# Value products of grouped query attention: one product for the two heads of a pair

## The chip, the cores and the metric

The program runs on one core of a Trainium2 chip. The metric is device time in microseconds, the median of the runs; lower is better. Engines go by the profile's names: PE is the matrix engine (PEld its weight loads), DVE the vector engine, ACT the scalar engine, POOL GpSimd, SP the engine whose queue issues the DMAs here.

## What is computed

Two layers over 512 latent tokens with 256 context tokens in front of them, model width 1024, all in fp32. Each layer projects its input with one large matrix, runs four mixers (a state-space scan S5, a short convolution, neighbourhood attention NA, grouped query attention GQA), gates each branch, projects it to the model width ("merge"), sums the branches, and projects the sum once more. In GQA there are 8 query heads of 64 and 2 key/value heads, so four query heads share the values of one key/value head:

```python
def block(i):                       # 128 queries, a window of 384 keys, and 256 context keys
    s_lat = jnp.where(ok, jnp.einsum("bqkgd,bskd->bkgqs", q_i, k_i) * scale, NEG_INF)
    s_ctx = jnp.einsum("bqkgd,bckd->bkgqc", q_i, k_ctx) * scale
    pr = jax.nn.softmax(jnp.concatenate([s_lat, s_ctx, sink_l], axis=-1), axis=-1)
    o = (jnp.einsum("bkgqs,bskd->bqkgd", pr[..., :span], v_i)
         + jnp.einsum("bkgqc,bckd->bqkgd", pr[..., span:span + n_ctx], v_ctx))
```

The last two lines are the value products that the change touches. Context queries see context keys only. Layer 0 computes latent and context outputs (768 tokens), layer 1 latent ones alone (512).

## The kernel before

**Arithmetic.** An fp32 product is made of three reduced-precision ones: each operand is split into a high part (an ACT cast, L229) and a low part (a DVE subtraction, L230), and hi x hi, hi x lo and lo x hi are summed in PSUM. The large projections ("dense" work) do this at L209: a unit is a weight tile of 128x1024 (`wraw`, two buffers, loaded by SP at L170), cast by ACT (`whi`, L177) and subtracted by DVE or POOL (`wlo`, L178); then come 24 matmuls of 512 columns into `pl` for the latent tokens, and in layer 0 another 24 of 256 columns into `pc` for the context.

**Attention.** `attend_` handles 128 queries of one head: logits into PSUM tile `S` (one buffer, shared with the merges), a bias and row maximum on DVE, the exponential on ACT (L579), normalisation on DVE, then PE transposes of the probabilities into `T` (two buffers, L590), split into `ph` and `pl_` (two buffers each). The value product follows at once: for each block of 128 keys three matmuls of 64 weight columns and 128 moving columns into `M` (L599), after which ACT copies `M` into `y` (L617). `gqa_tiles` goes head by head: for each of the two heads of a pair four latent blocks, in layer 0 two context blocks. There are 48 such head-blocks of GQA in layer 0 and 32 in layer 1; NA has as many.

**Order.** A layer's `front` weaves the attention tiles of eight pairs (m = 0 to 3 NA, 4 to 7 GQA) with dense units; a scheduler then sets each engine's order by priorities, with `attend` raised by `tile_prio` = 1500. In layer 0, `s5_prep` (DVE work for the S5 branch) is woven into pairs 6 and 7. After the last pair, `gate(7)` closes the front: POOL multiplies the gate with `y` (L414), ACT and DVE split it (`ghi`, `glo`), SP stores both to DRAM (L422, L423). The `back` begins with `merge`: SP loads the gated branches again as `gh` and `gl` (L1315, eight loads), PE multiplies them into `S` (L209, named `S<-gh`, `S<-gl`), DVE adds the result to `acc` (L1335), and since `S` has one buffer the second merge waits for that. In layer 0 the first steps of the S5 back (`sX`, `swin`, `sWO` on DVE, L1025 to L1043; their PE transposes L1060 and L1069) stand between the first and the second merge. SP runs its queue in order: the stores of `gate(7)`, weight loads, the S5 loads (`skl`, `smt`, `su`) and the `gh`/`gl` loads stand behind each other.

Of the kernel before, what the change touches and what calls it, by code (L numbers as in the profile page):

```python
# [12 lines left out]
F32R = mybir.dt.float32r  # L13
AF = mybir.ActivationFunctionType
OP = mybir.AluOpType
# [5 lines left out]
CTX = 256  # L21
# [9 lines left out]
C_BADA, C_G, C_CONVB, C_CONVW, C_NAQ, C_NAK, C_GQQ, C_GQK, C_SINK, N_COLS = 0, 24, 32, 36, 48, 49, 50, 51, 52, 60  # L31
B_S5, B_CONV, B_NA, B_GQA = 0, 1, 2, 3

NA_KEYS = [(0, (2, 3)), (1, (6, 7)), (3, (7, 8)), (4, (4, 5))]
# [88 lines left out]
class Net:  # L123
# [424 lines left out]
    def attend(self, *args):  # L548


        with self.tc.high_priority(offset=self.tile_prio):
            self.attend_(*args)

    tile_prio = 1500

    def attend_(self, pool, qs, kh, kl, v, qtok, k0, vbs, bias, sink, dst):
        nc = self.nc
        n = len(vbs) * 128
        S = self.ps.tile([128, 1024], F32, name="S")
# [19 lines left out]
        nc.scalar.activation(s[:, a:e], s[:, a:e], AF.Exp, bias=tn[:, 1:2], accum_out=tn[:, 2:3])  # L579
        nc.vector.reciprocal(tn[:, 3:4], tn[:, 2:3])  # L580
        nc.vector.tensor_scalar(s[:, a:640], s[:, a:640], tn[:, 3:4], None, op0=OP.mult)
        ph = pool.tile([128, 640], F32R, name="ph", bufs=2)
        pl = pool.tile([128, 640], F32R, name="pl_", bufs=2)
        vbs = (*vbs, 0, 1)
        nb = len(vbs)
        for b0 in range(0, nb, 4):
            b1 = min(nb, b0 + 4)
            T = self.ps.tile([128, 512], F32, name="T", bufs=2)
            for b in range(b0, b1):
                nc.tensor.transpose(T[:, (b - b0) * 128:(b - b0 + 1) * 128], s[:, a + b * 128:a + (b + 1) * 128], self.ident)  # L590
            c = slice(b0 * 128, b1 * 128)
            self.split(ph[:, c], pl[:, c], T[:, :(b1 - b0) * 128])
        o = self.ps.tile([128, 512], F32, name="M")
        i = 0
        for b in range(nb):
            vb = vbs[b]
            c = slice(b * 128, (b + 1) * 128)
            for w, p in ((slice(0, 64), ph), (slice(0, 64), pl), (slice(64, 128), ph)):
                last = nc.tensor.matmul(o[:64, :128], v[:, vb, w], p[:, c], start=i == 0, stop=i == 3 * nb - 1)  # L599
                i += 1  # L600
        self.last_pv = last.ins
        dst(o[:64, :128])

    def store_y(self, y, h, j, na):
        nc = self.nc
        part = y[h * 64:(h + 1) * 64]

        def f(o):
            a = CTX - self.base
            if j < 0:  # L610
                d = part[:, (j + 2) * 128:(j + 3) * 128]
            elif na:
                d = part[:, a:].rearrange("p (r b c) -> p b r c", r=8, b=8)[:, 2 * j:2 * j + 2]
                o = o.rearrange("p (b r c) -> p b r c", r=8, c=8)
            else:
                d = part[:, a + j * 128:a + (j + 1) * 128]
            nc.scalar.copy(d, o)  # L617
        return f

    def na_setup(self, pool):  # L620
        self.biases, self.nbias = [], 0
        for i in range(2):
            b = pool.tile([128, 640], F32, name=f"bias{i}")
            self.nc.gpsimd.memset(b[:, 384:], 0.0)
            self.biases.append(b)
# [9 lines left out]
    def na_tiles(self, l, pool, m, parts, A):  # L635
        nc = self.nc
        A["y"] = y = self.tp(pool, "y", bufs=2)
        for h in range(2):
            args = (pool, A["qs"][h], A["kh"][h], A["kl"][h], A["v"][:, :, h])
            for j in range(4):  # L640
                b = self.biases[self.nbias % 2]
                self.nbias += 1
                k0, vbs = NA_KEYS[j]
                nc.sync.dma_start(b[:, 128:384], self.ap["bias"][l, 2 * m + h, j])
                self.attend(*args, CTX + j * 128, k0, vbs, b[:, 128:], None, self.store_y(y, h, j, True))
                yield
            if "c" in parts:
                for j in (-2, -1):
                    self.attend(*args, (j + 2) * 128, 0, (), self.zeros, None, self.store_y(y, h, j, True))
                    yield  # L650
        self.dump(f"yna{l}{m}", y)

    def gqa_k(self, l, pool, A):
# [7 lines left out]
    def gqa_tiles(self, l, pool, m, parts, A):  # L661
        A["y"] = y = self.tp(pool, "y", bufs=2)
        kv = m // 2
        for h in range(2):
            sink = self.cols[:, l, C_SINK + 2 * m + h:C_SINK + 2 * m + h + 1]
            args = (pool, A["qs"][h], A["kh"][kv], A["kl"][kv], A["v"][:, :, kv])
            for j in range(4):
                k0, k1 = max(0, j - 1), min(4, j + 2)
                mask = self.gmask3 if j == 3 else self.gmask[:, 128 if j == 0 else 0:]
                self.attend(*args, CTX + j * 128, 2 * k0, range(2 + k0, 2 + k1), mask, sink, self.store_y(y, h, j, False))  # L670
                yield
            if "c" in parts:
                for j in (-2, -1):
                    self.attend(*args, (j + 2) * 128, 0, (), self.zeros, sink, self.store_y(y, h, j, False))
                    yield
        self.dump(f"ygq{l}{m}", y)

    def front(self, l, pool, parts):
# [784 lines left out]
```

## Time and profile before

| | |
|---|---|
| median of 3 runs | 2170.95 us (2165.61 to 2174.13) |
| the profiled execution: its own time, its span | 2171.66 us, 2169.9 us |
| PE busy, of the span | 2097.1 us, 97% |
| DVE, ACT, POOL busy | 62%, 41%, 15% |
| chain that ended last, share of PE | 65% |
| clock of PE granted, mean | 0.976 of full |

The page gives busy times, the span in slices, the chain of waits followed back from the last instruction, and groups of instructions by line. A matmul's duration in a timeline is longer than its distance to the next one, since matmuls overlap in the pipeline; what one costs the engine is that distance, called its slot below.

### The profile page before, as it was taken

How to read it: one execution, taken by the hardware profiler on the slowest of the kernel's cores; microseconds unless marked ns; L12 is line 12 of the kernel's file. 1: busy time of each engine (PE TensorE's matmuls, PEld its weight loads, DVE VectorE, ACT ScalarE, POOL GpSimd, SP SyncE). 2: the span in 40 equal slices, each digit the busy share in tenths (PEclk: the TensorE clock that was granted, in tenths of full speed). 3: DMA queues.
4: the chain of work that ended last, by engine and by line, in shares of the span. 5: the costliest groups of instructions: out<-in, count | busy, mean ns of one | idle time of the engine just before them, and what ended most of it. 6: DMA issues, size and time to landing. Idle time of an engine off the chain costs nothing.

```text
span 2169.9 us, 34654 instructions
## 1 busy us (share of the span) xinstructions
PE 2097.1 (97%) x12868; PEld 1792.5 (83%) x12868; DVE 1351.5 (62%) x2770; ACT 898.5 (41%) x1936; POOL 322.3 (15%) x326
## 2 busy tenths in 40 slices
PE   8899999899999999999799998999999999999999
PEld 3788888798898888888688887888888887778877
DVE  6476767579665777777457764555556655556543
ACT  3454444354643333333233345555545443223332
POOL 1722122232310000000000003222223300000000
PEclk9999999999999999999899998999999999999999
DMA  6453553532324565554164765444333328764452
GB/s 254 129 151 103 154 151 112 156 120 64 135 81 156 149 179 161 135 178 126 54 205 142 219 208 183 136 118 131 98 112 96 110 95 259 232 199 135 144 167 97
DMA packets 165773, 316.45 MB, mean 146 GB/s; under 512 B 59362, under 2 KB 83170, under 8 KB 164836
## 3 DMA queue, kind: packets, MB, share of 16 engines
q1 hardware_dynamic: 165604, 314.24, 47.1%
q8 instruction: 101, 1.65, 0.3%
q14 instruction: 68, 0.56, 0.1%
HBM read 214.09 MB, written 51.31 MB: 122 GB/s over the span
## 4 chain that ended last, share of the span: by engine, by line
PE 65%; DMA 6%; DVE 5%; ACT 2%; SPq 1%; issue 1%; POOL 0%; DVEq 0%; ACTq 0%; POOLq 0%
PE pl L209 34%; PE pc L209 10%; PE S L209 8%; PE M L599 3%; DMA s<-s 2%; PE T L590 2%; PE T L1069 1%; PE S L563 1%; PE S L565 1%; PE T L1143 1%; DMA gl<-gd 1%; DMA gd<-s 1%; PE M L478 1%; PE T L1060 1%; DMA s<-yd 1%
## 5 line engine op out<-in xcount | busy, mean ns | idle before, releaser
L209 PE MATMUL pl<-hh,whi 128*128 128x512 f32 x1312 | 526.5, 403 | 5.4 <-ACT hh L229 2.5
L209 PE MATMUL pl<-hh,wlo 128*128 128x512 f32 x1312 | 525.3, 400 | 6.1 <-DVE wlo L178 6.1
L209 PE MATMUL pl<-hl,whi 128*128 128x512 f32 x1312 | 525.0, 400 | 0.4 <-DVE hl L230 0.4
L177 ACT CAST whi<-wraw 128x512 fp32r<-128x512 f32 x440 | 272.4, 622 | 534.7 <-PE pl L209 190.5
L178 DVE TENSOR_TENSOR wlo<-wraw,whi 128x512 fp32r<-128x512 f32 x348 | 241.4, 696 | 185.0 <-ACT whi L177 178.1
L209 PEld LDWEIGHTS pl<-hh,wlo 128*128 128x128 f32 x1312 | 249.4, 190 | 60.9 <-DVE wlo L178 8.2
L209 PEld LDWEIGHTS pl<-hh,whi 128*128 128x128 f32 x1312 | 249.8, 191 | 56.2 <-ACT hh L229 3.7
L209 PEld LDWEIGHTS pl<-hl,whi 128*128 128x128 f32 x1312 | 249.6, 190 | 51.0 <-DVE hl L230 1.5
L209 PE MATMUL pc<-hh,whi 128*128 128x256 f32 x768 | 225.4, 294 | 10.4 <-ACT hh L229 5.0
L209 PE MATMUL pc<-hl,whi 128*128 128x256 f32 x768 | 223.0, 290 | 0.7 <-DVE hl L230 0.5
L209 PE MATMUL pc<-hh,wlo 128*128 128x256 f32 x768 | 222.2, 289 | 0.0
L178 POOL TENSOR_TENSOR wlo<-wraw,whi 128x512 fp32r<-128x512 f32 x92 | 128.0, 1394 | 314.0 <-ACT whi L177 273.5
L209 PEld LDWEIGHTS pc<-hh,whi 128*128 128x128 f32 x768 | 149.1, 194 | 19.4 <-ACT hh L229 6.0
L579 ACT ACTIVATE s<-s,stiny 128x512 f32<-128x512 f32 (+2 forms) x160 | 112.8, 705 | 112.3 <-DVE stiny L578 56.0
L209 PEld LDWEIGHTS pc<-hl,whi 128*128 128x128 f32 x768 | 149.2, 194 | 6.8 <-DVE hl L230 1.6
L599 PE MATMUL M<-ph,v 128*64 128x128 f32 x1216 | 147.2, 228 | 4.1 <-ACT y L617 1.8
L209 PEld LDWEIGHTS pc<-hh,wlo 128*128 128x128 f32 x768 | 149.3, 194 | 0.8 <-issue 0.4
L209 PE MATMUL S<-gh,whi 128*128 128x512 f32 (+1 forms) x384 | 139.0, 362 | 3.0 <-DVE mt L1335 1.6
L209 PE MATMUL S<-gl,whi 128*128 128x512 f32 (+1 forms) x384 | 137.5, 358 | 1.6 <-DMA gl<-gd 1.6
L209 PE MATMUL S<-gh,wlo 128*128 128x512 f32 (+1 forms) x384 | 137.2, 357 | 0.0
L599 PEld LDWEIGHTS M<-ph,v 128*64 128x64 f32 x1216 | 127.0, 138 | 11.7 <-ACT y L617 3.1
L229 ACT CAST ph<-T 128x512 fp32r<-128x512 f32 (+2 forms) x192 | 92.8, 497 | 56.5 <-PE T L590 49.7
(778 smaller groups left out, 3738.4 us busy)
## 6 DMA issues: line engine op xcount, KB each, us to landing
wraw<-wu SPq DMA_DIRECT2D x220, 512.0 KB
wada<-wada SPq DMA_DIRECT2D x40, 512.0 KB
s<-s SPq DMA_DIRECT2D x80, 192.0 KB
bias<-bias SPq DMA_DIRECT2D x64, 128.0 KB
kh<-qhi SPq DMA_DIRECT2D x40, 192.0 KB
kl<-qlo SPq DMA_DIRECT2D x40, 192.0 KB
gh<-gd SPq DMA_DIRECT2D x16, 384.0 KB
gl<-gd SPq DMA_DIRECT2D x16, 384.0 KB
```

The lines of the kernel that those rows point to most:

```text
L177: nc.scalar.copy(hi, raw[:, c])
L178: e.tensor_tensor(lo, raw[:, c], hi.bitcast(F32), op=OP.subtract)
L209: mm = nc.tensor.matmul(out[q], a[:, c], b[k][:, s], start=k + n == 0, stop=k == nk - 1 and n == 2)
L229: self.nc.scalar.copy(hi, src)
L478: nc.tensor.matmul(sums[:, 2 * b:2 * b + 2], sq[:, c:c + 128], self.blk1, start=True, stop=True)
L563: nc.tensor.matmul(S[:, 512 - n:512], qa, k[:, CTX + k0 * 64:CTX + k0 * 64 + n], start=i == 0, stop=i == 1)
L565: nc.tensor.matmul(S[:, 512:768], qa, k[:, :CTX], start=i == 0, stop=i == 1)
L579: nc.scalar.activation(s[:, a:e], s[:, a:e], AF.Exp, bias=tn[:, 1:2], accum_out=tn[:, 2:3])
L590: nc.tensor.transpose(T[:, (b - b0) * 128:(b - b0 + 1) * 128], s[:, a + b * 128:a + (b + 1) * 128], self.ident)
L599: last = nc.tensor.matmul(o[:64, :128], v[:, vb, w], p[:, c], start=i == 0, stop=i == 3 * nb - 1)
L1060: nc.tensor.transpose(o[:, g * 128:(g + 1) * 128], win[d][:, g].rearrange("p s i -> p (s i)"), self.ident)
L1069: nc.tensor.matmul(o[:16, g * 128:(g + 1) * 128], X[:, 0, d, g], WO[:, d, g, d:d + 8].rearrange("p k i -> p (k i)"), start=True, stop=True)
```

## The change

In GQA the two heads of a pair are done side by side, block by block: `gqa_tiles` now loops over the query block outside and the head inside, and after the second head one call (`values_`) does the value products of both. The weights are the high and low halves of the values together (128 columns), the moving operand is the probabilities of both heads together (256 columns), first their high part and then their low part: two matmuls for each block of keys instead of three for each head. Rows 0 to 63 of the result hold what came from the high values, rows 64 to 127 what came from the low ones (the product lo x lo is thereby added). ACT copies the first half of a head into `y` as before, and DVE then adds the second half (new, L631). `ph` and `pl_` become one tile each for the whole front, with two halves: a GQA pair uses both halves at once, NA alternates between them. The products of NA keep their form.

```diff
--- before.py
+++ after.py
@@ -551,9 +551,13 @@
         with self.tc.high_priority(offset=self.tile_prio):
             self.attend_(*args)
 
+    def values(self, *args):
+        with self.tc.high_priority(offset=self.tile_prio):
+            self.values_(*args)
+
     tile_prio = 1500
 
-    def attend_(self, pool, qs, kh, kl, v, qtok, k0, vbs, bias, sink, dst):
+    def attend_(self, pool, qs, kh, kl, half, qtok, k0, vbs, bias, sink):
         nc = self.nc
         n = len(vbs) * 128
         S = self.ps.tile([128, 1024], F32, name="S")
@@ -579,10 +583,8 @@
         nc.scalar.activation(s[:, a:e], s[:, a:e], AF.Exp, bias=tn[:, 1:2], accum_out=tn[:, 2:3])
         nc.vector.reciprocal(tn[:, 3:4], tn[:, 2:3])
         nc.vector.tensor_scalar(s[:, a:640], s[:, a:640], tn[:, 3:4], None, op0=OP.mult)
-        ph = pool.tile([128, 640], F32R, name="ph", bufs=2)
-        pl = pool.tile([128, 640], F32R, name="pl_", bufs=2)
-        vbs = (*vbs, 0, 1)
-        nb = len(vbs)
+        ph, pl = (t[:, half] for t in self.pt)
+        nb = len(vbs) + 2
         for b0 in range(0, nb, 4):
             b1 = min(nb, b0 + 4)
             T = self.ps.tile([128, 512], F32, name="T", bufs=2)
@@ -590,23 +592,33 @@
                 nc.tensor.transpose(T[:, (b - b0) * 128:(b - b0 + 1) * 128], s[:, a + b * 128:a + (b + 1) * 128], self.ident)
             c = slice(b0 * 128, b1 * 128)
             self.split(ph[:, c], pl[:, c], T[:, :(b1 - b0) * 128])
+
+    def values_(self, v, vbs, half, dsts):
+
+
+        nc = self.nc
+        ph, pl = self.pt
+        vbs = (*vbs, 0, 1)
         o = self.ps.tile([128, 512], F32, name="M")
-        i = 0
-        for b in range(nb):
-            vb = vbs[b]
+        for b, vb in enumerate(vbs):
             c = slice(b * 128, (b + 1) * 128)
-            for w, p in ((slice(0, 64), ph), (slice(0, 64), pl), (slice(64, 128), ph)):
-                last = nc.tensor.matmul(o[:64, :128], v[:, vb, w], p[:, c], start=i == 0, stop=i == 3 * nb - 1)
-                i += 1
+            if half is None:
+                for i, p in enumerate((ph, pl)):
+                    last = nc.tensor.matmul(o[:, :256], v[:, vb], p[:, :, c], start=b + i == 0, stop=b == len(vbs) - 1 and i == 1)
+                continue
+            for i, (w, p) in enumerate(((slice(0, 64), ph), (slice(0, 64), pl), (slice(64, 128), ph))):
+                last = nc.tensor.matmul(o[:64, :128], v[:, vb, w], p[:, half, c], start=b + i == 0, stop=b == len(vbs) - 1 and i == 2)
         self.last_pv = last.ins
-        dst(o[:64, :128])
+        for h, dst in enumerate(dsts):
+            dst(o[:, h * 128:(h + 1) * 128], half is None)
 
     def store_y(self, y, h, j, na):
         nc = self.nc
         part = y[h * 64:(h + 1) * 64]
 
-        def f(o):
+        def f(o, two):
             a = CTX - self.base
+            o, o2 = o[:64], o[64:]
             if j < 0:
                 d = part[:, (j + 2) * 128:(j + 3) * 128]
             elif na:
@@ -615,10 +627,13 @@
             else:
                 d = part[:, a + j * 128:a + (j + 1) * 128]
             nc.scalar.copy(d, o)
+            if two:
+                nc.vector.tensor_tensor(d, d, o2, op=OP.add)
         return f
 
     def na_setup(self, pool):
         self.biases, self.nbias = [], 0
+        self.pt = [pool.tile([128, 2, 640], F32R, name=n) for n in ("ph", "pl_")]
         for i in range(2):
             b = pool.tile([128, 640], F32, name=f"bias{i}")
             self.nc.gpsimd.memset(b[:, 384:], 0.0)
@@ -635,19 +650,23 @@
     def na_tiles(self, l, pool, m, parts, A):
         nc = self.nc
         A["y"] = y = self.tp(pool, "y", bufs=2)
+        half = 0
         for h in range(2):
-            args = (pool, A["qs"][h], A["kh"][h], A["kl"][h], A["v"][:, :, h])
-            for j in range(4):
-                b = self.biases[self.nbias % 2]
-                self.nbias += 1
-                k0, vbs = NA_KEYS[j]
-                nc.sync.dma_start(b[:, 128:384], self.ap["bias"][l, 2 * m + h, j])
-                self.attend(*args, CTX + j * 128, k0, vbs, b[:, 128:], None, self.store_y(y, h, j, True))
+            v = A["v"][:, :, h]
+            for j in (0, 1, 2, 3) + ((-2, -1) if "c" in parts else ()):
+                args = (pool, A["qs"][h], A["kh"][h], A["kl"][h], half)
+                if j >= 0:
+                    b = self.biases[self.nbias % 2]
+                    self.nbias += 1
+                    k0, vbs = NA_KEYS[j]
+                    nc.sync.dma_start(b[:, 128:384], self.ap["bias"][l, 2 * m + h, j])
+                    self.attend(*args, CTX + j * 128, k0, vbs, b[:, 128:], None)
+                else:
+                    vbs = ()
+                    self.attend(*args, (j + 2) * 128, 0, vbs, self.zeros, None)
+                self.values(v, vbs, half, (self.store_y(y, h, j, True),))
+                half = 1 - half
                 yield
-            if "c" in parts:
-                for j in (-2, -1):
-                    self.attend(*args, (j + 2) * 128, 0, (), self.zeros, None, self.store_y(y, h, j, True))
-                    yield
         self.dump(f"yna{l}{m}", y)
 
     def gqa_k(self, l, pool, A):
@@ -661,18 +680,18 @@
     def gqa_tiles(self, l, pool, m, parts, A):
         A["y"] = y = self.tp(pool, "y", bufs=2)
         kv = m // 2
-        for h in range(2):
-            sink = self.cols[:, l, C_SINK + 2 * m + h:C_SINK + 2 * m + h + 1]
-            args = (pool, A["qs"][h], A["kh"][kv], A["kl"][kv], A["v"][:, :, kv])
-            for j in range(4):
-                k0, k1 = max(0, j - 1), min(4, j + 2)
-                mask = self.gmask3 if j == 3 else self.gmask[:, 128 if j == 0 else 0:]
-                self.attend(*args, CTX + j * 128, 2 * k0, range(2 + k0, 2 + k1), mask, sink, self.store_y(y, h, j, False))
+        v = A["v"][:, :, kv]
+        for j in (0, 1, 2, 3) + ((-2, -1) if "c" in parts else ()):
+            k0, k1 = (max(0, j - 1), min(4, j + 2)) if j >= 0 else (0, 0)
+            mask = self.zeros if j < 0 else self.gmask3 if j == 3 else self.gmask[:, 128 if j == 0 else 0:]
+            vbs = range(2 + k0, 2 + k1)
+            for h in range(2):
+                sink = self.cols[:, l, C_SINK + 2 * m + h:C_SINK + 2 * m + h + 1]
+                qtok = CTX + j * 128 if j >= 0 else (j + 2) * 128
+                self.attend(pool, A["qs"][h], A["kh"][kv], A["kl"][kv], h, qtok, 2 * k0, vbs, mask, sink)
+                if h == 1:
+                    self.values(v, vbs, None, [self.store_y(y, i, j, False) for i in range(2)])
                 yield
-            if "c" in parts:
-                for j in (-2, -1):
-                    self.attend(*args, (j + 2) * 128, 0, (), self.zeros, sink, self.store_y(y, h, j, False))
-                    yield
         self.dump(f"ygq{l}{m}", y)
 
     def front(self, l, pool, parts):
```

In this case the scheduler sets the order anew, and so dense units move as well. At the end of layer 0's front PE has, before the change, the last value product and then the rest of a dense unit:

```order
L599 MATMUL M<-pl__7621,v 64x128
L599 MATMUL M<-ph,v 64x128
L209 MATMUL pc<-hh_77,whi 128x256
L209 MATMUL pc<-hl_85,whi 128x256
L209 MATMUL pc<-hh_77,wlo 128x256
L209 MATMUL pc<-hh_78,whi 128x256
```

Further on in the same order stands the place where PE first needs the S5 preparation (`swin`) while dense `pl` and merge matmuls alternate; 62 `pc` and 52 `pl` stand ahead of the first `S<-gh`, and 72 and 78 in all between the last value product and the second merge:

```order
L209 MATMUL pl<-hh_81,whi 128x512
L209 MATMUL pl<-hl_89,whi 128x512
L209 MATMUL S<-gh_7879,whi 128x512
L1060 MATMUL T<-kc,swin 128x128 x4
L209 MATMUL S<-gl_7881,whi 128x512
L209 MATMUL S<-gh_7879,wlo 128x512
L209 MATMUL pl<-hh_81,wlo 128x512
L209 MATMUL pl<-hh_82,whi 128x512
```

After the change 24 `pc` and 48 `pl` stand there, all ahead of the first merge, and this is where they end:

```order
L209 MATMUL pl<-hh_84,wlo 128x512
L209 MATMUL S<-gh_7353,whi 128x512
L209 MATMUL S<-gl_7355,whi 128x512
L209 MATMUL S<-gh_7353,wlo 128x512
L209 MATMUL S<-gh_7357,whi 128x512
L209 MATMUL S<-gl_7359,whi 128x512
L209 MATMUL S<-gh_7357,wlo 128x512
L209 MATMUL S<-gh_7361,whi 128x512
L209 MATMUL S<-gl_7363,whi 128x512
L209 MATMUL S<-gh_7361,wlo 128x512
L1079 MATMUL T<-kc,swin 128x128 x4
L209 MATMUL S<-gh_7365,whi 128x512
```

48 `pc` and 30 `pl` matmuls have moved to places ahead of the last value product, and the transposes of `swin` come after nine merge matmuls. At the end of layer 1's front PE has, before the change, this (the first of 48 `pl` matmuls follow the last value product, and the first merge is woven among the second half of them):

```order
L599 MATMUL M<-ph,v 64x128 x2
L599 MATMUL M<-pl__19102,v 64x128
L599 MATMUL M<-ph,v 64x128
L1143 MATMUL T<-su,sWT 128x96 x2
L209 MATMUL pl<-hh_77,whi 128x512
L209 MATMUL pl<-hl_85,whi 128x512
L209 MATMUL pl<-hh_77,wlo 128x512
L209 MATMUL pl<-hh_78,whi 128x512
```

After the change the last value products stand between bare transposes, and the first merge matmul follows the last of them:

```order
L592 MATMUL T<-kc,s 128x128 x4
L1162 MATMUL T<-su,sWT 128x96 x8
L607 MATMUL M<-ph,v 128x256
L607 MATMUL M<-pl__13552,v 128x256
L607 MATMUL M<-ph,v 128x256
L607 MATMUL M<-pl__13552,v 128x256
L607 MATMUL M<-ph,v 128x256
L607 MATMUL M<-pl__13552,v 128x256
L607 MATMUL M<-ph,v 128x256
L607 MATMUL M<-pl__13552,v 128x256
L209 MATMUL S<-gh_18362,whi 128x512
L209 MATMUL S<-gl_18364,whi 128x512
```

The 48 `pl` matmuls have moved to places ahead of the last value product, and no dense matmul is left between it and the second merge. After the second merge of layer 1 PE's order is the old one.

## Rows read from the trace of the kernel before

**Rows 1.** The page's parts 1 and 4: busy time by engine, and the chain.

```profile
PE 2097.1 (97%) x12868; PEld 1792.5 (83%) x12868; DVE 1351.5 (62%) x2770; ACT 898.5 (41%) x1936; POOL 322.3 (15%) x326
...
PE 65%; DMA 6%; DVE 5%; ACT 2%; SPq 1%; issue 1%; POOL 0%; DVEq 0%; ACTq 0%; POOLq 0%
```

**Rows 2.** The page's part 5: busy, mean ns of one | idle before.

```profile
L599 PE MATMUL M<-ph,v 128*64 128x128 f32 x1216 | 147.2, 228 | 4.1 <-ACT y L617 1.8
```

**Rows 3.** Timeline of PE, start us and duration: first and last of three runs.

```profile
560.39 0.28 PE L209 MATMUL pc<-hh,whi 128*128 128x256 f32 x1
...
561.34 0.28 PE L209 MATMUL pc<-hh,wlo 128*128 128x256 f32 x1
...
567.83 0.22 PE L599 MATMUL M<-ph,v 128*64 128x128 f32 x1
...
568.67 0.22 PE L599 MATMUL M<-ph,v 128*64 128x128 f32 x1
...
1784.33 0.39 PE L209 MATMUL pl<-hl,whi 128*128 128x512 f32 x1
...
1785.96 0.40 PE L209 MATMUL pl<-hh,wlo 128*128 128x512 f32 x1
```

**Rows 4.** Stretches: length, PE, PEld, DVE, ACT, POOL busy, clock, DMA share, GB/s.

```profile
413.00:677.00 264.00, 259.87 (x1920) 234.12 (x1918) 190.92 (x555) 134.37 (x367) 62.25 (x79) 0.99 0.30 98
480.00:520.00 40.00, 39.60 (x287) 35.68 (x286) 39.58 (x160) 17.88 (x46) 11.91 (x11) 1.00 0.19 65
689.00:711.00 22.00, 22.00 (x129) 18.75 (x128) 18.60 (x31) 8.13 (x17) 0.11 (x1) 1.00 0.90 295
1797.00:1806.00 9.00, 6.85 (x28) 4.97 (x27) 2.39 (x4) 3.20 (x5) 0.11 (x1) 0.96 1.02 313
```

**Rows 5.** Timeline, end of layer 0's front to the second merge, several engines.

```profile
676.89 0.22 PE L599 MATMUL M<-ph,v 128*64 128x128 f32 x1
...
677.15 0.26 ACT L617 COPY y<-M 64x128 f32<-64x128 f32 x1 [3.78 <-PE M L599]
...
688.98 0.29 DVE L1025 TENSOR_TENSOR sX<-smt,skl 128x128 f32<-128x128 f32 x1 [6.25 <-DMA smt<-s5m]
689.19 0.68 DVE L178 TENSOR_TENSOR wlo<-wraw,whi 128x512 fp32r<-128x512 f32 x1
...
699.50 0.68 DVE L1043 TENSOR_TENSOR swin<-swin,spw 128x512 f32<-128x512 f32 x1
...
705.39 0.76 DVE L1043 TENSOR_TENSOR sWO<-sWO,spw 128x576 f32<-128x576 f32 x1
...
708.51 1.02 DVE L1335 SCALAR_TENSOR_TENSOR acc<-mt,S 128x256 f32<-128x256 f32 x2 [2.36 <-PE S L209]
...
710.69 0.50 PE L209 MATMUL S<-gh,whi 128*128 128x512 f32 x1
```

**Rows 6.** Timeline, end of layer 1's front to the second merge, several engines.

```profile
1788.17 0.22 PE L599 MATMUL M<-ph,v 128*64 128x128 f32 x1
...
1791.84 0.47 SPq L1315 DMA_DIRECT2D gh<-gd  x1
...
1805.24 0.79 PE L209 MATMUL S<-gh,whi 128*128 128x512 f32 x1 [0.78 <-DVE acc L1335]
```

**Rows 7.** PE's timeline and the stretch after one of its waits.

```profile
528.99 0.58 PE L565 MATMUL S<-kh,qs 128*128 128x256 f32 x1 [2.85 <-DVE stiny L569]
...
533.62 0.63 PE L209 MATMUL pl<-hh,whi 128*128 128x512 f32 x1
534.04 0.63 PE L209 MATMUL pl<-hl,whi 128*128 128x512 f32 x1
...
529.00:535.00 6.00, 5.86 (x26) 4.98 (x27) 6.00 (x20) 4.68 (x13) 0.00 (x0) 0.50 0.29 66
```

**Rows 8.** Groups by line and shape: busy, mean ns; and one instruction of DVE.

```profile
L229 ACT CAST ph<-T 128x512 fp32r<-128x512 f32 x128 | 74.7, 586 | 48.4 <-PE T L590 45.0 <-PE M L599 2.1 <-DVE pl__14992 L230 0.5
...
1779.61 0.69 DVE L230 TENSOR_TENSOR pl__19102<-T,ph 128x512 fp32r<-128x512 f32 x1 [2.77 <-ACT ph L229]
```

## The prediction

> **What bounds the kernel now.** I read the page's busy times and its chain first. PE is busy in 97% of the span and holds 65% of the chain; no other engine comes near [rows 1]. So PE work that goes away is time, unless PE then waits. The group of the value products has 147.2 us busy [rows 2], but durations overlap in the pipeline, so the next view is PE's timeline, for what one instruction takes to the next: 15 value products start from 567.83 to 568.67, 0.84/14 = 0.060 us each; nine `pc` matmuls, 128 weight columns and 256 moving ones, from 560.39 to 561.34, 0.95/8 = 0.119; eight `pl` matmuls from 1784.33 to 1785.96, 1.63/7 = 0.233 [rows 3]. Then the places where PE leans on others: a stretch where DVE is full (39.58 of 40 us [rows 4]) and PE waits 2.85 us soon behind it [rows 7], and the ends of the two fronts. There the chain value product, copy, POOL multiplication, split, store, load, merge is long, and dense work has to cover it. In layer 0 PE is busy for every microsecond of 689 to 711, so the cover is enough today; in layer 1 it is not quite, 6.85 of 9 us [rows 4].
>
> **What goes.** GQA has 80 head-blocks. Counted in the order, their value products are 960 before (528 in layer 0, 432 in layer 1) and 320 after (176 and 144); those of NA stay. 960 x 0.060 = 57.6 us go, 320 x 0.119 = 38.1 come. The new form has the weight and moving shape of a `pc` matmul, so I take its slot. PE saves 19.5 us: 10.7 in layer 0, 8.8 in layer 1.
>
> The Trainium skill ("TensorE: Matmul & The Clock Gate", section "Back-to-back issue gap") gives about 81 ns for each matmul of 128 columns in a stream of weight loads and matmuls. By it the removed work would be 960 x 0.081 = 77.8 us and the saving 39.7. The row of this very instruction says 0.060 [rows 3], so the sum goes by that.
>
> **What comes.** 80 additions on DVE of 64x128. The nearest row, a 128x128 two-operand instruction, takes 0.29 us [rows 5]: 23.2 us in all, 13.9 in layer 0. DVE is 62% busy [rows 1], and mostly this costs nothing, because PE's dense work hides it. Where DVE is full, 480 to 520, it does not: that stretch is 40 of the front's 264 us of attention, so it gets about 40/264 [rows 4] x 13.9 = 2.1 us more DVE work, while PE there gets 1.6 shorter. If DVE sets the pace there, PE waits 0 to 3.7 us more; I take 1.5, a little under the middle, since over all 264 us DVE has 73 to spare [rows 4]. The single `ph` and `pl_` tile lets a new pair's split begin only after the products of the last pair; a split not covered costs a cast and a subtraction, 0.59 + 0.69 = 1.28 [rows 8]. I take one of them in layer 0, 1.2, with 0 and 3 as bounds.
>
> **What moves: layer 0.** The saving can stay only if the end of the front does not wait, and the order says that it will. 30 `pl` and 48 `pc` matmuls, 7.0 + 5.7 = 12.7 us, now stand ahead of the last value product. That product therefore ends at 677.1 [rows 5] - 10.7 + 12.7 + 1.5 + 1.2 = 681.8. Behind it only 48 `pl` and 24 `pc` are left, 11.2 + 2.9 = 14.1 us (before 78 and 72: 18.2 + 8.6 = 26.8), and after nine merge matmuls, 2.1 us, PE comes to the transposes of `swin`. What do these need? Before, `sX` starts 11.9 us after the last value product, behind `smt` in SP's queue, and that behind the stores of the final gate [rows 5]. Two things make this later: `y` is now finished by copy, add, copy, add, 0.26 + 0.29 twice [rows 5] instead of one copy, about 1.0 us with the hand-offs and only partly parallel; and SP now issues `smt` behind one more weight load, whose buffer two DVE subtractions free, 2 x 0.69 [rows 8], about 1.5. So `sX` starts at 14.4. From there the first `swin` took 11.2 us before, to 700.18, and in it three weight subtractions of about 0.6 like that of 689.19 [rows 5], 1.8, which now stand ahead: 9.4. PE has `swin` at 23.8, having been out of work since 16.2: a hole of almost 8 us. To the last `sWO` DVE needs the 5.3 us that it needed before without its weight subtraction, then 1.0 for `acc` [rows 5], while PE does the other 15 merge matmuls. The second merge starts at 14.4 + 9.4 + 5.3 + 1.0 = 30.1 after 681.8, at 711.9. Before, it started at 710.69 [rows 5]. From there on PE's remaining work differs only by layer 1's. So layer 0 gives +1.2 in place of -10.7: the gain is turned into waiting. Bounds: -2, if none of the 1.5 and 1.2 and half of the longer queue is paid, to +4.
>
> **Layer 1.** 48 `pl`, 11.2 us, move ahead of the last value product there, against 8.8 saved: +2.4. Ahead of it three pairs now run almost bare, transposes, splits and value products with one dense matmul among them. Each hand-off of transposes to the split and back is a cast and a subtraction, 1.28 us, and 0.3 for the last transposes and the semaphores: about 1.6, three times, 4.8 (bounds 2 and 7). The last product so ends at 1788.4 [rows 6] + 1.2 + 2.4 + 4.8 = 1796.8. Before, the second merge started 16.85 us after that end, with 11.2 us of dense work in between, and at its end PE waited for `acc` [rows 6]; most of that time is a chain that does not get shorter when PE has nothing to do: 3.4 us to the first load of `gh` [rows 6], then loads at 313 GB/s with the DMA engines full [rows 4]. The final `y` is 1.0 later here too; dense work does not delay the first merge any more, up to 2.5 us less. I take 16.6 (15.3 to 17.9). The second merge starts at 1813.4 against 1805.24: +8.2 in all, layer 0's 1.2 included.
>
> **The clock.** After the 2.85 us wait at 528.99 PE ran at a granted clock of 0.50, the level of 1.2 GHz, and `pl` matmuls came at 0.43 in place of 0.23 until 535 (534.04 - 533.62 = 0.42): 6 us with about 3 lost [rows 7]. Two larger holes now open. The second is followed by a stretch that runs at a low clock already [rows 4], and part of the first's slow time falls into work that waits for DVE anyway. 0 to 6, taken as 2.5.
>
> **Sum.** 2171.66, the profiled execution, + 8.2 + 2.5 = 2182.4. It lay 0.7 above the median, so 2181.7.
>
> **Rivals.** *The gain arrives whole.* The holes stay shut because the chain is shorter than its rows: PE never waited in 689 to 711, so the 11.9 us to `sX` may hold slack. 2171.66 - 19.5 - 0.7 = 2151.5. Against it: DVE sat idle 6.25 us until `smt` landed [rows 5], so that part was no slack, and 14 us of cover are less than 23. 7%. *Half of it holds.* The bare pairs of layer 1 overlap better (2 instead of 4.8), the chain there takes 15.3, layer 0 loses just its gain, the clock costs nothing: 8.2 - 1.2 - 2.8 - 1.3 = 2.9 more, 2173.9, and with the lower bound of layer 0 two less: 2172. 35%. *Slower, on the other side of no change:* the mechanism is PE's low clock behind both holes, from the point where PE waits longer than the 2.85 us of the row. At 0.50, 6 us of each handover are stretched, and the bare pairs of layer 1, alternating with waits, stay at that level as well: their 25 value products and 32 transposes, some 5 us, take 5 more. 2181.7 + 3.5 + 5 = 2190. 15%. *The change does not do what it says:* a product with 128 weight columns and 256 moving ones costs the slots of three of 64 and 128, 0.18. The `pc` rows speak against it [rows 3]. Nothing is saved and both last value products come 10.7 and 8.8 later: 2181.7 + 19.5 = 2201. 3%. My forecast has 40%, between 2176 and 2187.
>
> The Trainium skill, in the section "Loop structure matters more than you think" of the same page, has it that the order of the loops decides whether PE keeps its high clock, and that copying a result out does no harm as long as the next matmuls follow at once. Here they do not follow at once after the change. By that rule the third rival would have the most of it; the row at 528.99 agrees with it for one wait [rows 7], and no row shows bare pairs.
>
> **How the numbers follow.** About 0.5%, 10.9 us, is what a measurement of this kernel tells from no change: faster is below 2160.1, slower above 2181.8. Faster has the first rival and a tail of the second: 0.11. Slower has half of the forecast, the third and the fourth rival and some of what lies between: 0.44. The same: 0.45, most of the second and half of the forecast. The range leaves out the first and the fourth rival with a little of the others' ends: 2162 to 2191.
>
> **What would show it.** In the profile after: value products of 128x256 at 0.119 apart, and PE's busy time about 20 us shorter; a PE wait of 7 to 10 us some 16 us after layer 0's last value product, released by DVE (`swin`); the second merge of layer 0 at 710 to 713; waits on the split in the last three pairs of layer 1; the second merge there 6 to 10 us later than 1805, with waits for `gh` and `gl`; stretches at a clock of 0.50 behind them. The prediction is wrong if the value products take another slot, if PE does not wait for `swin`, or if the loads of `gh` and `gl` are there when PE comes to the first merge of layer 1.

## The result, and the profile after

The changed kernel takes 2181.18 us in the median of 8 runs (2178.77 to 2194.66), the kernel before 2168.58 (8 runs, 2163.95 to 2174.13). The ratio is 1.0078, 95% interval 1.0061 to 1.0095: slower by 0.8%, and 2181.7 was forecast, with a range of 2162 to 2191. The number came out right. Two of the terms that made it did not, and their errors cancelled, which was luck; the experiments below are about that. The profiled executions take 2171.66 us before and 2178.77 after, the shortest of the eight after: of the 12.6 us between the medians the traces show 7.1.

Parts 1 and 4 of the page after:

```profile
PE 2078.0 (95%) x12228; PEld 1766.0 (81%) x12228; DVE 1374.3 (63%) x2850; ACT 894.9 (41%) x1936; POOL 319.4 (15%) x326
...
PE 75%; DVE 9%; DMA 7%; issue 4%; ACT 3%; SPq 2%; POOL 1%; DVEq 0%; ACTq 0%; POOLq 0%
```

The two new instructions among the groups by line and shape (count | busy, mean ns | idle before and releaser):

```profile
L607 PE MATMUL M<-ph,v 128*128 128x256 f32 x160 | 42.2, 289 | 0.4 <-ACT ph L229 0.3
L631 DVE TENSOR_TENSOR y<-y,M 64x128 f32<-64x128 f32 x80 | 23.3, 291 | 18.0 <-ACT y L629 16.0
```

PE's busy time fell by 19.1 us against [rows 1], and its slots had said 19.5. That the two agree so closely is partly chance: five profiles with the old products, in the kernel before and in experiments below, show PE busy for 2090.2 to 2097.1 us. DVE's rose by 22.8, 80 additions of 0.291. The span rose by 7.1 (2169.9 to 2177.0). So PE gained 26 us of idle time. PE's largest waits at the two hand-overs and behind the second one, and the second merges (timeline; the bracket is the idle time before the instruction and what ended it):

```profile
688.02 0.79 PE L209 MATMUL S<-gh,whi 128*128 128x512 f32 x1 [4.59 <-DMA gh<-gd]
690.69 0.79 PE L209 MATMUL S<-gl,whi 128*128 128x512 f32 x1 [1.88 <-DMA gl<-gd]
701.39 0.50 PE L209 MATMUL S<-gh,whi 128*128 128x512 f32 x1
...
1800.21 0.79 PE L209 MATMUL S<-gh,whi 128*128 128x512 f32 x1 [7.35 <-DMA gh<-gd]
1808.51 0.50 PE L209 MATMUL S<-gh,whi 128*128 128x512 f32 x1 [0.78 <-DVE acc L1354]
1840.03 0.50 PE L209 MATMUL pl<-hh,wlo 128*128 128x512 f32 x1 [4.16 <-DVE wlo L178]
```

The lines of 701.39 and 1808.51 are the second merges; they answer to 710.69 [rows 5] and 1805.24 [rows 6]. In layer 0 the merge comes 9.3 us earlier than before, in layer 1 3.3 later: 12.6 us are lost between the two, and more behind, until the span ends 7.1 later. The stretches around the hand-overs (length, busy time of PE, PEld, DVE, ACT, POOL, granted clock, DMA share, GB/s):

```profile
688.00:697.00 9.00, 6.73 (x14) 3.57 (x14) 8.90 (x13) 1.15 (x2) 0.00 (x0) 0.50 0.98 349
1620.00:1660.00 40.00, 34.41 (x173) 28.15 (x171) 25.14 (x62) 19.12 (x44) 9.66 (x14) 0.96 0.28 86
1793.00:1808.00 15.00, 6.75 (x12) 2.96 (x12) 1.50 (x4) 3.78 (x9) 1.49 (x3) 0.66 0.82 253
```

Both hand-overs are holes now, with a granted clock of 0.50 in the first merge of layer 0 and of 0.66 in that of layer 1. The line of 1620 to 1660 was not foreseen: 5.6 us of idle time in the middle of layer 1's attention.

### The profile page after: what moved, and what is told of

Its sections match the earlier page's. It is cut to its first block, busy times and chain, and to the rows that moved or that the text cites. A ratio compares the mean times of both kernels' runs of the same rounds, so it can differ in the third digit from the quotient of the medians.

```text
span 2177.0 us, 33498 instructions
## 1 busy us (share of the span) xinstructions
PE 2078.0 (95%) x12228; PEld 1766.0 (81%) x12228; DVE 1374.3 (63%) x2850; ACT 894.9 (41%) x1936; POOL 319.4 (15%) x326
## 4 chain that ended last, share of the span: by engine, by line
PE 75%; DVE 9%; DMA 7%; issue 4%; ACT 3%; SPq 2%; POOL 1%; DVEq 0%; ACTq 0%; POOLq 0%
PE pl L209 39%; PE pc L209 12%; PE S L209 8%; DMA s<-s 3%; PE T L592 2%; PE M L610 2%; PE T L1088 1%; PE S L569 1%; PE S L567 1%; PE M L607 1%; DVE wadaj L325 1%; DMA gl<-gd 1%; PE M L478 1%; DVE wlo L178 1%; PE T L1162 1%
## 5 line engine op out<-in xcount | busy, mean ns | idle before, releaser
L583 ACT ACTIVATE s<-s,stiny 128x512 f32<-128x512 f32 (+3 forms) x160 | 112.6, 704 | 120.4 <-DVE stiny L579 56.6
L229 ACT CAST ph<-T 128x512 fp32r<-128x512 f32 (+1 forms) x192 | 93.0, 496 | 75.6 <-PE T L592 65.4
L592 PE MATMUL T<-kc,s 128*128 128x128 f32 x608 | 99.9, 278 | 5.0 <-DVE s L585 1.6
L325 DVE SCALAR_TENSOR_TENSOR wadaj<-wada,siluc 128x1024 f32<-128x1024 f32 x72 | 93.7, 1302 | 10.3 <-DMA wada<-wada 10.3
```

Source lines behind the costliest of these rows:

```text
L229: self.nc.scalar.copy(hi, src)
L325: nc.vector.scalar_tensor_tensor(j, w, 1.0, self.siluc[:, v], op0=OP.mult, op1=OP.mult, accum_out=m[:, b, v:v + 1])
```

## The experiments

Times are medians; ratios are against the kernel before on the same chip. The theory at the start: the loss is the hand-overs that lost their cover.

**Cover given back.** In `merge_z` the dense matmuls of the first three merge units are ordered behind the last value product, in layer 0, in layer 1, and in both.

```diff
-        z = self.proj(l, MERGE + br * 8 + m, parts)
+        w = self.unit(l, MERGE + br * 8 + m)
+        late = br == B_CONV and m < 3 and l == 0     # l == 1; no condition on l
+        with self.tc.issue_after(self.last_pv) if late else nullcontext():
+            z = self.dense(w, 0, KD, self.hh, self.hl, parts)
```

> The kernel after, with the three dense units of the first merge in layer 0 held on PE behind the layer's last value product (72 pl and 72 pc matmuls ahead of the first merge matmul in place of 48 and 24). Theory (the loss is the uncovered hand-over, not the products): PE's waits for gh and gl at layer 0's hand-over (4.6 + 1.9 us, and the slow clock behind them, some 3) go away, the second merge starts 5 to 10 us earlier than 701.4, and the time falls from 2181 to 2171 to 2176. Rival (the attention tiles need the dense work as cover themselves): the waits only move ahead of the last value product, the time stays within 2 us of 2181.

> The same in layer 1 only: 72 pl matmuls ahead of the first merge matmul in place of none. Theory: the wait for gh (7.4 us), the slow clock in the first merge and the wait for wlo at 1840 (4.2 us) go, while the last pairs stay as bare as they are or get a little barer (0 to 5 us more): the time falls by 6 to 12 us, to 2169 to 2175. Rival: the dense units are missing ahead of the last value product as much as they help behind it, the time stays within 3 us of 2181.

> Both layers at once. Theory: the two hand-overs are independent, the gains add: 2160 to 2169, that is, at or below the kernel before (2168.6), since the saving of the products (19.5 us of PE time) then shows at least in part. Rival: no change from 2181 or at most the better one of the two alone.

Measured: layer 0 2185.95, ratio 1.0082 (1.0061 to 1.0103); layer 1 2176.17, 1.0056 (1.0031 to 1.0081); both 2187.34, 1.0081 (1.0057 to 1.0106). The waits for `gh` at the covered hand-overs were gone, and the theory still lost: layer 0 gained nothing, layer 1 some 5 us by the medians, a little less than was expected and not clear of noise (the interval overlaps with that of the change, 1.0061 to 1.0095), both together nothing. In layer 0 the second merge did come earlier, at 694.25 in place of 701.39, as was expected; but 24 `pl` matmuls now stood behind it, and at the third merge, with the same work of PE done, the times are 710.74 and 710.31. The trace of the run on layer 1 shows more, in the stretches ahead of the last value product and behind it:

```profile
1740.00:1780.00 40.00, 26.17 (x146) 21.72 (x145) 31.12 (x83) 21.76 (x55) 6.18 (x12) 0.87 0.17 57
1780.00:1804.00 24.00, 24.00 (x110) 19.88 (x109) 5.77 (x10) 9.32 (x18) 1.51 (x3) 0.93 0.67 229
```

Behind, PE is now full; ahead, the last GQA pair runs with two dense `pl` matmuls (129 in the kernel before, 113 in the kernel after) and leaves PE idle for 13.8 us. Holding cover back takes it from the attention tiles. There is too little dense work left for both, so the question is where it was spent.

**The additions alone.** Taken out of the kernel after (the line `nc.vector.tensor_tensor(d, d, o2, op=OP.add)`), and put into the kernel before:

```diff
             nc.scalar.copy(d, o)
+            if not na:
+                nc.vector.tensor_tensor(d, d, self.zeros[:64, :128], op=OP.add)
```

> The kernel after without the 80 additions on DVE: the half of the result that comes from the low part of the values is computed and left out of y. It prices the additions with all that hangs on them (y is finished by two copies again). Theory: they cost about 1 us at each hand-over and 0 to 3 us where DVE is full, so 2176 to 2181, and the holes at the hand-overs stay. Rival (DVE is the new bound, the additions are the loss): at or below 2169.

> The kernel before with 80 additions on DVE, 64x128 each, one behind each GQA copy (zeros are added). It prices the additions alone. Theory from the run without additions (they cost 14.7 us there, DVE being full in parts of layer 0's GQA and the y chain longer at both hand-overs): 2175 to 2182. Rival (the run without additions gained by another order, not by less DVE work): 2166 to 2171.

Without them the time is 2166.5, ratio 1.0004 (0.9989 to 1.0020): 14.7 us less than with them, below the 2176 of my theory. With them the kernel before takes 2174.4, 0.31% (0.15 to 0.47%) more, about 7 us, just under what was expected. Both are more than the 1.5 and twice 1.0 of the prediction. The rival was right that the additions matter. That DVE is the only new bound is not borne out: without the additions the products still save nothing, though PE has less to do (busy 2078.2, as after); the time is that of the kernel before.

**Product form against loop order.** The loop order and the tiles of the change with the old three products for each head, and the loop order alone in the kernel before:

```diff
                 if h == 1:
-                    self.values(v, vbs, None, [self.store_y(y, i, j, False) for i in range(2)])
+                    for i in range(2):
+                        self.values(v, vbs, i, (self.store_y(y, i, j, False),))
```

> The kernel after with the old form of the value products: pair by pair, one ph and pl_ tile, products of both heads late, but three products of 64 weight and 128 moving columns for each head, and no additions. It undoes the product form and the additions and keeps the loop order and the tiles. Without additions and with the new products the time was 2166.5. Theory now (loop order and tiles cost what the products save): 2166.5 + 19.5 = 2186, say 2180 to 2190. Rival (order and tiles are free, the new products save nothing): 2164 to 2170.

> The kernel before with its GQA loops exchanged alone: query block outside, head inside; products, tiles and stores as before. Theory (in head-by-head order one half of the next pair's queries can be loaded while the other head is still at work, by pairs it can't, so that the pauses between pairs grow from 17 to 27 us as in the kernel after): slower by 5 to 19 us, 2172 to 2186. Rival (it is the shared ph and pl_ tile, or the late products, that hold attention up): within 3 us of 2167.

Measured: 2165.28, ratio 1.0002 (0.9983 to 1.0021), and 2169.3, 1.0017 (0.9997 to 1.0037). My theory fell twice: loop order, shared tile and late products cost nothing that can be told from zero. So the three steps are: loop order and tiles nothing; new products, without additions, nothing, though PE has 19.5 us less work by the slots; additions 7 to 15 us. The single profiles with and without the new products suggest where their gain goes: the second merge of layer 0 comes 6.5 us earlier with them (700.37, 693.83), and from there to the second merge of layer 1 it takes 6.8 us longer (1101.67, 1108.44). What takes it away in layer 1?

**Where it goes: the next pair's queries.** In layer 1, attention of a pair needs the queries (`qs`) that a dense unit and a chain of casts, rotations and DMAs make while the pair before is at work. From the last logits of a GQA pair to the first of the next one, in layer 1, first pair to second: before 1627.77 to 1644.36, after 1612.79 to 1639.29.

```profile
1627.77 0.28 PE L565 MATMUL S<-kl,qs 128*128 128x256 f32 x1
1644.36 0.39 PE L563 MATMUL S<-kh,qs 128*128 128x256 f32 x1 [2.06 <-DMA qs<-qlo]
...
1688.39 0.28 PE L563 MATMUL S<-kh,qs 128*128 128x256 f32 x1
...
1621.53 0.61 ACT L486 COPY qsq<-qtiny 128x512 f32<-128x512 f32 x1
1637.20 0.62 ACT L229 CAST qhi<-qraw 128x512 fp32r<-128x512 f32 x1 [2.07 <-DVE qraw L511]
```

That was the kernel before: PE's logits (the line of 1688.39 begins the third pair) and the two steps of ACT that bound the query chain (`qsq` is the copy before the transposes, `qhi` the cast before the DMAs). The kernel after:

```profile
1612.79 0.28 PE L569 MATMUL S<-kl,qs 128*128 128x256 f32 x1
1639.29 0.28 PE L567 MATMUL S<-kh,qs 128*128 128x256 f32 x1
...
1693.38 0.28 PE L567 MATMUL S<-kh,qs 128*128 128x256 f32 x1
...
1614.46 0.61 ACT L486 COPY qsq<-qtiny 128x512 f32<-128x512 f32 x1
1631.49 0.62 ACT L229 CAST qhi<-qraw 128x512 fp32r<-128x512 f32 x1 [3.15 <-DVE qraw L511]
```

The pause is 16.6 us before and 26.5 after; between the second pair and the third it is 16.9 and 28.0. The first pair begins 12 us earlier after the change (1585.1 against 1597.1), the third 5 us later (1693.4 against 1688.4). The pauses are long in the run without additions too (26.0 and 22.1) and short with the old products (16.7 and 12.3): they come with the new products. Counted from the second merge of layer 0, the third pair begins 977.7 us later before the change, 977.0 with the old products, 994.0 without additions and 992.0 in the kernel after: by then all that layer 1 loses is lost. The query chain is hardly longer (15.7 us between the two steps before, 17.0 after), but it starts 6.2 us ahead of the pair's last logits before the change and 1.7 us behind them after it, and PE fills the pauses with dense units: 16.8 and 19.4 us of them, counted in the order by their slots, stand ahead of the second and third pair where 11.0 and 13.5 stood. These are missing later on. Test: give the next pair's queries, in layer 1, the priority of the attention tiles.

```diff
# shortened
+    def gqa_q(self, l, pool, m, parts, A):
+        if self.q_first is not None:                 # 1500 in layer 1
+            with self.tc.high_priority(offset=self.q_first):
+                self.gqa_q_(l, pool, m, parts, A)    # the old gqa_q; its qk_turn likewise
```

> The kernel after, layer 1 only: the projection of the next pair's queries and its turn get the priority of the attention tiles (offset 1500). In PE's order 10.5 us of dense work in place of 16.8 then stand ahead of the second GQA pair and 14.7 in place of 19.4 ahead of the third. Theory (in layer 1 attention waits for the next pair's queries, 27 and 28 us from the last logits of a pair to the first of the next in place of 17, PE runs dense work meanwhile and lacks it at the end): the pauses fall to 15 to 20 us, the second merge of layer 1 comes 4 to 8 us earlier, the time is 2171 to 2177. Rival (the pauses don't matter, since PE is at work in them): within 3 us of 2181.

> The control: the kernel before with the queries' priority of layer 1 raised in the same way. Theory (before, PE is the bound there, and the pauses of 17 us are covered to the end): within 3 us of 2166. Rival (early queries help any version): 3 to 8 us less.

Measured: 2163.82, ratio 1.0001 (0.9985 to 1.0017), some 17 us below the change alone and more than the theory's 4 to 10; the control 2162.47, 0.9989 (0.9974 to 1.0004). By its median the control is 3.5 us faster, just outside what the theory allowed and within the rival's range; by its interval no change is not excluded, nor are 5 us. The 17 us are far more than that. In the trace the pause is 14.7 us and the one after it 20.6, and the third pair begins 977.8 us behind layer 0's second merge, as before the change:

```profile
1613.90 0.28 PE L569 MATMUL S<-kl,qs 128*128 128x256 f32 x1
1628.59 0.28 PE L567 MATMUL S<-kh,qs 128*128 128x256 f32 x1
...
1785.99 0.79 PE L209 MATMUL S<-gh,whi 128*128 128x512 f32 x1 [7.28 <-DMA gh<-gd]
1795.75 0.79 PE L209 MATMUL S<-gh,whi 128*128 128x512 f32 x1 [0.78 <-DVE acc L1371]
```

The second merge of layer 1 comes at 1795.75, 12.8 us earlier than after. The hand-over's wait for `gh` is as long as it was (7.28), so it is not what made the difference of these 17 us. That they come from the shorter pauses, and not from something else in the new order, is what the traces suggest; no run separates the two. Leaving out the additions and raising the queries' priority each take the whole loss of 12.6 us away. The distance from the 19.5 us of the slots to that loss is 32, and 15 and 17 make 32; but no run has both, so that they add is not shown. The cover is tried again in this order:

**Queries early, cover and stores.** The same with one merge unit (the third) held behind the last value product of layer 1, and then with `y` stored by two copies and after them two additions.

```diff
# shortened: store_y then copies where lo is False and adds where it is True
-        for h, dst in enumerate(dsts):
-            dst(o[:, h * 128:(h + 1) * 128], half is None)
+        for lo in (False, True)[:1 + (half is None)]:
+            for h, dst in enumerate(dsts):
+                dst(o[:, h * 128:(h + 1) * 128], lo)    # copies first, then additions
```

> The same, and in layer 1 the third dense unit of the first merge is held behind the last value product (48 pl matmuls ahead of the first merge matmul in place of none). Theory: both parts of layer 1's loss shrink, the wait for gh of 7.4 us goes, 2164 to 2171. Rival (whatever is taken from ahead of the last value product is missing there): 2171 to 2179, no better than the queries alone.

> The same again, and y is stored by two copies and then two additions (before: copy, addition, copy, addition, where the second copy waits for the first addition). Theory (part of what the additions cost is the longer way of y and the longer hold on M): 2 to 5 us less than the run without it. Rival (the additions cost by DVE's load alone): within 1.5 us of it.

Measured: 2157.01, ratio 0.9968 (0.9944 to 0.9992), and 2154.63, 0.9955 (0.9939 to 0.9972). With the queries early the cover pays more than was expected: the wait for `gh` is gone, and five of the six times lie below the lowest of the ten without it (2160.16). The medians differ by 2.4 us, within what was expected, but the two intervals overlap, so the gain of the store order is not shown by the times. The traces show one wait that it may shorten. `M` has one buffer, and the last value products of layer 1 wait for the additions on it, first with copies and additions by turns, then with the copies first:

```profile
1769.14 0.36 PE L607 MATMUL M<-ph,v 128*128 128x256 f32 x1 [2.12 <-DVE y L631]
```

```profile
1761.51 0.55 PE L607 MATMUL M<-ph,v 128*128 128x256 f32 x1 [0.88 <-DVE y L633]
```

The last version is below both kernels, by 0.45% below the kernel before and by 7.8 us below the control. The kernel before was not run with the cover, so how much of this the product form pays is not separated.

**An experiment that told nothing.** The low halves were copied by ACT into the idle bias tiles and added once for each pair.

> The kernel after with the low halves copied by ACT into a tile of their own (the two bias tiles, idle in GQA) and added once for each pair: 8 latent and 4 context additions on DVE, about 5 us in place of 23, and 80 more ACT copies of 0.26 us. Theory (the number of DVE additions is what costs): 2167 to 2172, near the run without additions. Rival (the longer way of y at the hand-over costs, and it is longer still here by one wide addition): 2178 to 2184.

It took 2186.02, 1.0086 (1.0057 to 1.0115), above both ranges, and for a reason not weighed: in layer 0 the S5 preparation uses the same two tiles as work space, and ACT stood behind it. The trace's waits of PE around that hand-over:

```profile
663.35 0.58 PE L209 MATMUL pc<-hh,whi 128*128 128x256 f32 x1 [10.79 <-ACT mt L1332]
686.07 0.58 PE L209 MATMUL pc<-hh,whi 128*128 128x256 f32 x1 [11.61 <-ACT mt L1332]
```

Whether fewer, wider additions would cost less stays open.

## Why the prediction was right in its number, and where it was wrong

**What goes: right.** The new products start 0.12 us apart (below, the second and the last of eight in layer 1's last pair; 0.71 us for six steps), the slot taken from `pc`. PE's busy time fell by 19.1 us for the 19.5 forecast; against the five profiles with old products it is 12 to 19. The old products were 0.060 us apart [rows 3]. The 81 ns of the Trainium skill ("TensorE: Matmul & The Clock Gate", section "Back-to-back issue gap"), which would have made it 39.7, do not hold here.

```profile
1791.87 0.28 PE L607 MATMUL M<-pl__13552,v 128*128 128x256 f32 x1
...
1792.58 0.28 PE L607 MATMUL M<-pl__13552,v 128*128 128x256 f32 x1
```

**What comes: mis-sized.** An addition takes 0.291 us, as its nearest row had it. But I priced the additions at DVE's load (1.5) and the last store of a front (1.0 each), and they cost 7 us in the kernel before and 14.7 in the kernel after. This is the term of the sum that was sized too small. Against the run without them, the profile of the kernel after is 7.6 us later at the second merge of layer 0 (693.83, 701.39), 1.3 us shorter from there to that of layer 1, and 5.4 us longer behind it, where no addition stands. I had not priced the tile `M`, which copy, addition, copy, addition hold; but the profile of the kernel after has no wait of PE's value products for an addition: such waits stand in the five runs that hold dense work behind a last value product, 0.9 to 5.0 us in all. How much of the cost is DVE's time, how much `M` and how much another order of the scheduler was not separated.

**Layer 0: the chain right, the sum wrong.** `sX` started 14.5 us after the last value product (14.4 forecast), the first `swin` was done at 24.1 (23.8), the second merge came at 32.0 (30.1):

```profile
669.13 0.28 PE L607 MATMUL M<-pl__441,v 128*128 128x256 f32 x1
...
683.92 0.29 DVE L1044 TENSOR_TENSOR sX<-smt,skl 128x128 f32<-128x128 f32 x1 [4.76 <-DMA smt<-s5m]
...
692.87 0.68 DVE L1062 TENSOR_TENSOR swin<-swin,spw 128x512 f32<-128x512 f32 x1
```

But the last product ended at 669.4 and not at 681.8, so that the merge came at 701.39 and not at 711.9. The 1.5 and 1.2 us of extra waits were not paid in sum: PE's waits from 400 to 668 are 4.8 us, against 8.3 before, though 3.4 of the 4.8 are new waits on the split (`pl__441`). The wait of 2.85 us with the slow stretch behind it [rows 7] went away, since the order there is another. Much of the rest is the clock: over the stretches of 20 us up to 680, length times what the granted clock lacks to 1 sums to 29 us before and 19 after, an estimate of the time lost at most. Of this much is chance, since the control run, with the same order in layer 0 as before, has 22; its last product ends at 671.4 and its second merge comes at 705.0. Against that run layer 0 gained 3.6 us, against [rows 5] 9.3. The step that failed is "the gain is turned into waiting": a hole opened, about 7 us and a slow merge as forecast, but the gain ahead of it, in part the clock's, was larger than what it took. The releaser was wrong too, by the prediction's own sign: PE waited for `gh` and `gl`, in the queue behind `su`, and had `swin` by the time it came to it.

**Layer 1: the direction right, the size wrong.** Forecast were +7.0 us from layer 0's second merge to that of layer 1; measured are 12.6 against [rows 5, 6]. Behind that merge the kernel after takes 3.8 us more (364.7, 368.5), with a wait of 4.16 for a weight tile at 1840; but the control takes 368.5 there too, so the profiles do not show that as a cost of the change. The bare last pairs and the hole of 7.35 us were there, and the chain from the last product to the second merge took 15.6 us (16.6 forecast). Missing in the sum are the pauses ahead of the second and third pair. I had walked the order at its end, where the cover was gone, and not asked where it had been used. The rows of before show the pause's source: the second pair waits 2.06 us for its queries there, at 1644.36.

**The clock: right in its net, by chance.** Stretches at the lower level moved to the hand-overs (0.50 in 688 to 697, 0.66 in 1793 to 1808), as forecast, and others, ahead of layer 0's last value product, went away. The mean granted clock is 0.975 after and 0.976 before. In the run with cover in layer 1 the bare pair, with PE busy for 26.17 of 40 us, has 0.87 in 1740 to 1780. The Trainium skill (the same page, section "Loop structure matters more than you think") has it that the loops decide whether PE keeps its high clock, and that a long wait between matmuls costs it; the bare pair agrees.

**The rival "half of it holds"** came nearer in layer 0, with a loss of nothing and -2 as its bound where 3.6 to 9.3 us were gained. The third, bare pairs at a slow clock, had little of it: the granted clock is 1.00 in 1740 to 1775 and 0.91 from there to 1793. The sum held because layer 0 was better than forecast and layer 1, with what follows it, worse by about as much: 10.5 and 9.4 us against [rows 5, 6], 4.8 and 5.6 against the control.

## What to carry to other kernels

Work taken from a full engine is time only if every chain that was hidden behind that work has something else to hide behind; ask this at each place where a stage ends, and also in the middle, where the next stage's inputs are made. When a scheduler orders the program, a missing cover at the end is best looked for upstream: count the filler work between stages in the order before and after, and find what the stage was waiting for while it was spent. An accumulation moved out of PSUM onto another engine can cost time even where that engine has room on average: here 23 us of additions on an engine busy for 63% of the span cost 7 to 15.

## What the runs showed of the hardware

The same instructions of PE in the same order (layer 0's front, in the kernel before and in the control with early queries in layer 1) took 677.1 and 671.4 us, with PE busy for 644.50 and 638.87 us at a mean granted clock of 0.96 and 0.97:

```profile
0.00:677.10 677.10, 644.50 (x4333) 550.78 (x4334) 456.61 (x1174) 321.92 (x782) 180.75 (x152) 0.96 0.42 132
```

```profile
0.00:671.40 671.40, 638.87 (x4333) 545.20 (x4334) 456.47 (x1174) 321.09 (x782) 180.66 (x152) 0.97 0.42 133
```

So a difference of 6 us in one stage between two profiles says nothing of a change here; it is more than half of the range of the whole times of the kernel before (2163.95 to 2174.13).
